# A two-layer streaming encoder step on one core: the row shift of the new values goes through a DRAM scratch instead of an SBUF to SBUF transfer

## The chip, the cores and the metric

One NeuronCore of a Trainium2 chip runs the whole step as one program. The metric is the device time of one execution in microseconds (us), lower is better. It is given as the median of several runs; the profile is one further execution.

## What is computed

Two groups of frames, 2048 prompt frames and 64 sample frames, pass through layer A (attention in a band), then layer B (stick-breaking attention over all earlier keys), each with a gated output projection. Layer B's keys and values come from one projection of the stream between the layers; they are outputs as well:

```
kb, vb = split(rms_norm(x, norm_kv) @ w_kv)              # 2112 x 1024 each
z = q @ k.T * SCALE;  mask = k_pos < q_pos
w = where(mask, exp(log_sigmoid(z) + later), 0)          # later: sum of log_sigmoid(-z) over the keys behind
o = w @ v
y = rms_norm(x + (o * silu(gate)) @ w_out, norm_f)
```

The kernel sums the sticks by parts: it multiplies the running products by the difference of neighbouring value rows, v[t-1] - v[t], and adds the last row at the end. For that it needs each value row beside the row above it. Row t-1 lies in another SBUF partition than row t (a tile holds 128 frames in 128 partitions), so the rows must be moved by one partition; this move is what the change concerns. Row 0 of the prompt has zeros above it, and the first sample frame has the last row of the cache.

## The kernel before

`projections` runs once for each layer, and in each it goes through two halves of the prompt (frames 0 to 1023 with the sample, then 1024 to 2047). Each half has a **value stage** and then a **product stage**.

- The value stage makes V with frames on partitions. A tile is 128 frames (tile 16: the 64 sample frames), and V is made in two halves of 512 columns. `values` does one tile and one half: 24 matmuls into a PSUM bank `ps_v` (16 for the sample tile), one of five banks. The first half of the prompt has 18 such steps, the second 16. Ahead of the product the tile is loaded (`xt`), normed, turned by the TensorE (`ps_tr`) and parted into a high and a low part (`x_own`, in the second half also `big`, `bigl`). In the first pass of the stage, or the second, `mix` forms sums of quarters of x on POOL, DVE and ACT for the product stage.
- The product stage makes K, Q and the gate, transposed, with Strassen-like products (`pair`: seven products of 12 matmuls into `ps_x`, `ps_z`, `ps_y`, which use the same five banks as `ps_v`). `natural` turns finished K chunks back with TensorE (`ps_n`, through `kn`) and writes them to the output `b_k_p`. Staging jobs (cache keys, `stage_diff` for the cache's value differences, the output weights `stage_w_out`) are spread over it.

In layer A `values` splits the PSUM bank straight into `vs` and stores it (`v_a`). In layer B each step does this, on SP unless said otherwise: ACT copies the bank to `vn` (four buffers); `vn` goes to the output `b_v_p` (L413); 127 rows of `vn` go one partition down into `vps` in SBUF (L418); the last row goes to the DRAM scratch `v_raw` (L419), and the row above the tile comes back from it into `vps` row 0 (L425); DVE subtracts `vn` from `vps`; ACT and DVE split the difference into `vs`; `vs` is stored to `v_b` (L396). `vps` has two places, used by turns. The last weight forms of the stage's end (`t4`) take over the place of `vps`.

The order of instructions on each engine is set by the tile framework's scheduler at compile time, unless `order.on` is set, in which case instructions made through the wrapped engines keep the program's order. Waits are put on semaphores, and an engine's queue is strictly in order. SP issues nearly all DMAs of these stages.

Of the kernel before, what the change touches and what calls it, by code (L numbers as in the profile page):

```python
# [16 lines left out]
P = 128  # L17
# [106 lines left out]
def encoder_step(ctx: ExitStack, tc: tile.TileContext, a: dict, o: dict):  # L124
# [143 lines left out]
    def projections(L, x_of, begin, w_v, cv, gv, out_v, jobs, first, prompt, sample, stages):  # L268
        with ExitStack() as own, ExitStack() as beside, ExitStack() as early:
# [98 lines left out]
            marker = {}  # L368

            def values(hf, half, i, t, vws, pool, vps):  # L370
                r0, n = TOK[t]
                xh, xl = xs[hf]
                c = r0 % HALF
                ps = psum.tile([P, CH], F32, name="ps_v", tag="mm", bufs=5)
                out = ps[:n]
                if n == NS:
                    for k in range(NK):
                        mm(ps, x_new[:, k], vws[k][0], start=(k == 0), stop=False)
                        mm(ps, x_new[:, k], vws[k][1], start=False, stop=(k == NK - 1))
                    out = pool.tile([P, CH], F32, name="vn", tag="vn", bufs=VN[L])[:n]  # L380
# [12 lines left out]
                def store(src, to):  # L393
                    vs = pool.tile([P, 8, 2, DH], F32R, name="vs", tag="vs", bufs=2)
                    copied = split(vs[:n, :, 0, :], vs[:n, :, 1, :], src.rearrange("p (h d) -> p h d", d=DH))
                    to(  # L396
                        f32(lay[L]["v"][r0 : r0 + n, heads]),
                        f32(vs[:n]).rearrange("p h s d -> p h (s d)"),
                    )
                    return copied  # L400

                if L == "a":
                    marker[hf, half, i] = store(out, nc.scalar.dma_start)
                dst = out_v(t)
                if dst is None:
                    return
                vn = out
                if n == P:
                    vn = pool.tile([P, CH], F32, name="vn", tag="vn", bufs=VN[L])
                    copied = act.activation(vn, out, AF.Copy)  # L410
                    if L == "b":
                        marker[hf, half, i] = copied
                nc.sync.dma_start(dst[:, cols], vn)  # L413
                if L == "a":
                    return

                prev = vps[i % 2]
                nc.sync.dma_start(prev[1:n], vn[: n - 1])  # L418
                nc.sync.dma_start(vraw[r0 + n : r0 + n + 1, cols], vn[n - 1 : n])  # L419
                if t == 0:  # L420
                    gps.memset(prev[0:1], 0.0)
                elif n == NS:
                    nc.sync.dma_start(prev[0:1], a["cache_b_v"][PAST - 1 : PAST, cols])
                else:
                    nc.sync.dma_start(prev[0:1], vraw[r0 : r0 + 1, cols])  # L425
# [46 lines left out]
            def pair(hf, kind, c0, hp, forms, pool, between):  # L472
# [10 lines left out]
                def plain(ps):  # L483
                    c = pool.tile([P, CH], F32, name="c", tag="c", bufs=CS[L])
                    act.activation(c, ps, AF.Copy)
                    return c

                def leave(b, t0, src):
                    at = slice(r0 + t0 * CH, r0 + t0 * CH + CH)
                    hl = pool.tile([P, 2, CH], F32R, name="hl", tag="hl", bufs=4)  # L490
# [5 lines left out]
                    put(L, kind, hp + b, at, hl)  # L496
                    row = hf * HALF + t0 * CH - first
                    if kind == "k" and row >= 0:
                        natural(pool, src, 0, P, 4, prompt[row : row + CH, (hp + b) * P : (hp + b) * P + P])

                def new_frames():
                    ps = bank("ps_q")[:, : 2 * P]
# [27 lines left out]
                        else:  # L530
                            put(L, kind, hp + b, at, hl[:, b])

                x, y, z = (None,) * 3
# [16 lines left out]
                leave(1, 0, u2)  # L550
                between(3)
                times(x, mixed(hf, 3), t3, False)
                dve.tensor_tensor(c5, x, c5, ALU.add)
# [3 lines left out]
                times(y, quarter(hf, 1, 0), w21, True)  # L557
                dve.tensor_tensor(c1, y, c1, ALU.add)
                leave(0, 0, c1)
                between(5)  # L560
                times(x, quarter(hf, 1, 1), t4, False)
                if kind == "k" and hf * HALF + CH - first >= 0:
                    leave(0, 1, plain(x))
                else:
                    leave(0, 1, x)
                between(6)

            def all_pairs(hf, todo, forms, raws, pool, begun, staging, events):
# [10 lines left out]
                for i, (kind, w, c0, g, hp) in enumerate(todo):  # L579
# [19 lines left out]
                            x()  # L599

                    pair(hf, kind, c0, hp, forms, pool, between)

            def slot(x):
                return x.rearrange("p (i k c) -> p i k c", i=2, k=4)
# [15 lines left out]
            ]  # L620


            seq = [*range(NK), len(TOK) - 1]
            with tc.tile_pool(name=f"v0_{L}", bufs=1) as pool:
                tmp = [x.rearrange("p k (i c) -> p (k i) c", i=2)[:, i] for x in big_parts(F32, (1, 2)) for i in range(4)]
                vps = two_places() if L == "b" else None
# [17 lines left out]
                for i, t in enumerate(seq):  # L644
                    if i + 2 < len(seq):
                        parted(seq[i + 2], turned(seq[i + 2], xts(seq[i + 2])))
                    if i >= 4 and i < 8:
                        mix(0, i - 4, [tmp[0], tmp[4 + i - 4], tmp[1], tmp[2]])
                    values(0, 0, i, t, vws, pool, vps)
                vws = [x for j in range(4) for x in two_blocks(1, j, ring(j), vw(pool))]  # L650
                forms = raws = None
                for i, t in enumerate(seq):
                    values(0, 1, i, t, vws, pool, vps)
                    if 4 <= i < 8:
                        x = tmp[i].rearrange("p (k t) -> p k t", k=4)
                        split(*into(0, 3, i - 4), x)
# [10 lines left out]
                    if i in (5, 6):  # L667
                        steps.pop(0)()
                        steps.pop(0)()
                t4 = opool.tile([P, 2, 4, P], F32R, name="t4", tag="og", bufs=1)  # L670


# [8 lines left out]
            last, seq1, fetched = len(todo[0]) - 1, [*range(NK, 2 * NK)], {}  # L681

            def fetch(part):
                if part == 0:
# [24 lines left out]
            with tc.tile_pool(name=f"v1_{L}", bufs=1) as pool:  # L709
                vps = two_places() if L == "b" else None  # L710
                where = [ahead, ahead, pool]
                for i, t in enumerate(seq1):
                    if i + 2 < NK:
                        home = where[(i + 2) % 3]
                        parted(seq1[i + 2], turned(seq1[i + 2], normed(seq1[i + 2], home, ahead, 1 if home is pool else 2)))
                    values(1, 0, i, t, vws, pool, vps)
                vws = []
                for j in range(4):
                    vws += two_blocks(1, j, "xr", vw(ahead if j < 2 else pool))
# [3 lines left out]
                for i, t in enumerate(seq1):  # L723
                    if i in (0, 2, 4, 6):
                        mix(1, i // 2, tmp)
                    values(1, 1, i, t, vws, pool, vps)
                    if i == 5:
                        raws = [raw_tiles()]
                        b1 = [opool.tile([P, 2, 4, P], F32R, name=f"b1{x}", tag="oh", bufs=2) for x in "hl"]
# [1 line left out]
                        load, scale, _ = weights_of(*todo[1][0], raws[0], [b1, None, None])  # L731
                        load()
                        scale()
                b2 = [opool.tile([P, 2, 4, P], F32R, name=f"b2{x}", tag="ol", bufs=2) for x in "hl"]
            early.close()
            own_forms = beside.enter_context(tc.tile_pool(name=f"st1_{L}", bufs=1))
# [35 lines left out]
        )  # L772


    def stage_diff(t, half, pool):
        cols, heads = slice(half * CH, half * CH + CH), slice(half * 8, half * 8 + 8)
        cur = pool.tile([P, CH], F32, name="vcur", tag="vr", bufs=2)
        prev = pool.tile([P, CH], F32, name="vprev", tag="vp", bufs=2)
        r0 = t * P
        cache = a["cache_b_v"]  # L780
        nc.sync.dma_start(cur, cache[r0 : r0 + P, cols])
        if t:
            nc.sync.dma_start(prev, cache[r0 - 1 : r0 + P - 1, cols])
        else:
            gps.memset(prev, 0.0)
            for x, m in ((0, 112), (112, 15)):
                nc.sync.dma_start(prev[x + 1 : x + 1 + m], cache[x : x + m, cols])

        gps.tensor_tensor(prev, prev, cur, ALU.subtract)
        vs = pool.tile([P, 8, 2, DH], F32R, name="vs", tag="vs", bufs=2)  # L790
        split(vs[:, :, 0, :], vs[:, :, 1, :], prev.rearrange("p (h d) -> p h d", d=DH))
        nc.sync.dma_start(f32(lay["b"]["v"][T + r0 : T + r0 + P, heads]), f32(vs).rearrange("p h s d -> p h (s d)"))


    def stage_w_out(k, half, pool):
# [580 lines left out]
    diffs = [partial(stage_diff, t, i) for t in range(PAST // P) for i in range(2)]  # L1376
    outs_b = [partial(stage_w_out, k, half) for k in range(NK) for half in range(2)]
    staged += keys_b[:8]
    staged_b = [x for i in range(16) for x in (keys_b[8 + i], diffs[16 + i])] + keys_b[24:]
# [18 lines left out]
    with (  # L1398
# [170 lines left out]
        0,  # L1569
        o["b_k_p"],  # L1570
        o["b_k_s"],
        [staged_b, outs_b],
    )

    with (
# [284 lines left out]
```

## Time and profile before

| what | value |
|---|---|
| timed runs | 3604.8 us median (3601.3 to 3606.26, 3 runs) |
| profiled execution, its own time | 3597.26 us |
| its span | 3595.5 us |
| mean granted TensorE clock | 0.947 |
| PE busy / DVE / ACT / POOL | 89% / 63% / 52% / 47% |
| layer B's first value stage, from its first `ps_v` | 1423.0 us |
| layer B's second value stage, from its first `ps_v` | 1992.5 us |

The page's strip of 40 slices shows each engine's busy tenths over time. The windows view gives busy time in chosen stretches, the waits view who waited for whom, the chain of waits the work that ended last, and the timeline every instruction with its start and length. "SPq" is the DMA issue on SP's queue; the length of a "DMA" piece in the chain is from its issue to its landing. Nearly all instructions carry the line of a helper, L113, so groups are told apart by the names of their tiles.

### The profile page before, as it was taken

To read this page: it belongs to the slowest core of one execution; us is meant where nothing else is said; L and a number is where in the kernel's file an instruction comes from. 1 tells how busy PE (TensorE), PEld (TensorE's weight loads), DVE (VectorE), ACT (ScalarE), POOL (GpSimd) and SP (SyncE) were. 2 spreads that over 40 slices of the span, in tenths; PEclk is the share of its full clock that TensorE was granted. 3 is DMA by queue.
4 is the path that set the end of the run, shared out by engine and by line. 5 is a ranking of instruction groups with operands and counts; after the bars stand their busy time and mean duration, and the time that the engine had idled before them with its cause. 6 is when DMAs were issued, how large, how long until landed. Compare 5 with 4: busy or idle time off the path is not lost.

```text
span 3595.5 us, 52143 instructions
## 1 busy us (share of the span) xinstructions
PE 3190.8 (89%) x16760; PEld 2650.4 (74%) x16760; DVE 2247.6 (63%) x3944; ACT 1873.4 (52%) x3743; POOL 1695.6 (47%) x2377
## 2 busy tenths in 40 slices
PE   8999999899989999552999662799999999999999
PEld 6778877688878987441778542578888887888877
DVE  6575466377777743321655322458887788888883
ACT  4445444488877742211544311446666666666662
POOL 4345267256555521311544211424447777777771
PEclk9999999999999999775999876899999999999999
DMA  4776457588999845222988322797683548554423
GB/s 160 249 252 208 149 212 255 170 231 230 258 249 250 225 136 164 82 86 102 344 303 308 137 85 83 270 273 225 187 219 123 146 134 248 148 148 141 123 70 124
DMA packets 470707, 674.72 MB, mean 188 GB/s; under 512 B 60051, under 2 KB 257203, under 8 KB 470434
## 3 DMA queue, kind: packets, MB, share of 16 engines
q1 hardware_dynamic: 425346, 607.95, 55.2%
q10 hardware_dynamic: 45088, 63.45, 5.2%
q8 instruction: 133, 2.18, 0.3%
q14 instruction: 140, 1.15, 0.1%
HBM read 412.51 MB, written 250.18 MB: 184 GB/s over the span
## 4 chain that ended last, share of the span: by engine, by line
PE 31%; DMA 11%; DVE 6%; issue 4%; ACT 2%; POOL 2%; SPq 2%; ACTq 0%; POOLq 0%; DVEq 0%
PE acc L113 6%; PE z L113 6%; PE wt L113 5%; DMA vps<-vn 5%; PE ps_j L113 5%; PE ps_x L113 3%; DMA v_raw<-vn 3%; PE ps_o L113 3%; DVE s L113 2%; DVE pl L113 2%; PE ps_z L113 2%; SPq L419 1%; PE ps_y L113 1%; POOL wraw L113 1%; DMA q<-q_b 1%
## 5 line engine op out<-in xcount | busy, mean ns | idle before, releaser
L113 DVE TENSOR_TENSOR pl<-wt,ph 128x512 fp32r<-128x512 f32 (+1 forms) x864 | 552.0, 655 | 109.4 <-ACT ph L113 105.9
L113 ACT ACTIVATE ph<-wt 128x512 fp32r<-128x512 f32 (+1 forms) x864 | 484.7, 577 | 192.4 <-PE wt L113 178.4
L113 PE MATMUL wt<-ident,s 128*128 128x128 f32 x3472 | 550.1, 274 | 9.4 <-DVE pl L113 7.4
L113 PEld LDWEIGHTS wt<-ident,s 128*128 128x128 f32 x3472 | 417.1, 140 | 84.1 <-DVE pl L113 13.4
L113 ACT ACTIVATE f<-z 128x512 f32<-128x512 f32 (+4 forms) x680 | 355.0, 535 | 191.6 <-PE z L113 129.4
L113 POOL TENSOR_TENSOR s<-f,s 128x256 f32<-128x256 f32 x416 | 360.7, 868 | 101.7 <-DVE s L113 93.6
L113 PE MATMUL z<-kt,q 128*128 128x512 f32 (+3 forms) x1280 | 372.7, 378 | 5.4 <-DMA q<-q_b 2.6
L113 PE MATMUL acc<-ph,vt 128*128 128x512 f32 (+3 forms) x1088 | 374.2, 379 | 3.6 <-ACT ot L113 2.4
L113 PE MATMUL acc<-pl,vt 128*128 128x512 f32 (+3 forms) x1088 | 362.9, 367 | 8.9 <-DVE pl L113 8.5
L113 POOL TENSOR_TENSOR two<-f 128x256 f32<-128x256 f32 x416 | 259.5, 626 | 151.5 <-ACT f L113 136.9
L113 DVE TENSOR_TENSOR_SCAN s<-two,s,own 128x256 f32<-128x256 f32 x408 | 300.3, 739 | 33.5 <-POOL two L113 32.0
L113 POOL TENSOR_SCALAR s<-s,rc 128x640 f32<-128x640 f32 (+5 forms) x264 | 201.2, 767 | 240.8 <-DVE rc L113 140.9
L113 PE MATMUL ps_x<-x_own,t 128*128 128x512 f32 x864 | 221.7, 405 | 68.1 <-DVE t L113 48.5
L113 PEld LDWEIGHTS z<-kt,q 128*128 128x128 f32 x1280 | 220.0, 190 | 36.1 <-ACT f L113 9.8
L113 PEld LDWEIGHTS ps_x<-x_own,t 128*128 128x128 f32 x864 | 163.2, 192 | 110.2 <-ACT c L113 62.8
L113 DVE TENSOR_TENSOR vps<-vps,vn 128x512 f32<-128x512 f32 (+1 forms) x34 | 23.5, 692 | 341.5 <-DMA vps<-vn 291.8
L113 DVE CUSTOM_DVE_ANT_0 s<-z,bias 128x640 f32<-128x640 f32 (+4 forms) x256 | 184.8, 733 | 71.4 <-PE wt L113 54.2
L113 PEld LDWEIGHTS acc<-pl,vt 128*128 128x128 f32 x1088 | 193.7, 190 | 41.6 <-DVE pl L113 25.9
L113 DVE TENSOR_TENSOR_SCAN s<-f,own 128x128 f32<-128x128 f32 (+4 forms) x264 | 202.4, 788 | 29.6 <-ACT f L113 29.2
L113 PEld LDWEIGHTS acc<-ph,vt 128*128 128x128 f32 x1088 | 196.7, 190 | 26.2 <-ACT ph L113 5.4
L113 POOL TENSOR_TENSOR wraw<-wraw 128x512 f32<-128x512 f32 x96 | 146.5, 1539 | 146.9 <-DVE b2l L113 77.8
L113 PE MATMUL ps_o<-big,oh 128*128 128x512 f32 x544 | 213.9, 393 | 0.0
(246 smaller groups left out, 7462.7 us busy)
## 6 DMA issues: line engine op xcount, KB each, us to landing
vt<-v_b SPq DMA_DIRECT2D x80, 512.0 KB
v_b<-vs SPq DMA_DIRECT2D x64, 512.0 KB
q<-q_a SPq DMA_DIRECT2D x128, 256.0 KB
q<-q_b SPq DMA_DIRECT2D x128, 256.0 KB
vt<-v_a SPq DMA_DIRECT2D x48, 512.0 KB
kt<-k_b SPq DMA_DIRECT2D x96, 256.0 KB
keys<-k_a SPq DMA_DIRECT2D x80, 256.0 KB
v_a<-vs ACTq DMA_DIRECT2D x32, 512.0 KB
```

The source lines that it names most:

```text
L113: ins = op(*args, **kwargs)
L419: nc.sync.dma_start(vraw[r0 + n : r0 + n + 1, cols], vn[n - 1 : n])
```

## The change

Three things change; the computation stays the same.

- In layer B `values` writes the whole tile `vn` to `v_raw`, at rows 1 + r0 and on, in place of the last row alone. Nothing is moved between partitions in SBUF. The step leaves two closures, `load` and `less`, in a list; `steps_on`, called after each `values`, calls a tile's `load` (read rows r0 to r0 + 127 of `v_raw` into `vps`) one tile later and its `less` (subtract, split, store) two tiles later, both in program order. What is left is called at the end of the stage.
- For the last two tiles of the second column half in each stage (tiles 7 and 16, then 14 and 15) `values` does no difference at all. `stage_diff` does them as staging jobs in the product stage, reading both `vn` rows and the rows above from `v_raw`; they stand first in the staging lists.
- `natural` is called one product later: `leave` puts it in the list `rows`, and `pair` takes one after its first, fifth, sixth and seventh products (the next pair's too).

```
-                nc.sync.dma_start(prev[1:n], vn[: n - 1])
-                nc.sync.dma_start(vraw[r0 + n : r0 + n + 1, cols], vn[n - 1 : n])
-                if t == 0:
-                    gps.memset(prev[0:1], 0.0)
-                elif n == NS:
-                    nc.sync.dma_start(prev[0:1], a["cache_b_v"][PAST - 1 : PAST, cols])
-                else:
-                    nc.sync.dma_start(prev[0:1], vraw[r0 : r0 + 1, cols])
-                dve.tensor_tensor(prev[:n], prev[:n], vn, ALU.subtract)
-                store(prev[:n], nc.sync.dma_start)
+                nc.sync.dma_start(vraw[1 + r0 : 1 + r0 + n, cols], vn)
+                if half and t in seqs[hf][-2:]:
+                    return
+                def load():
+                    if t == 0:
+                        gps.memset(prev[0:1], 0.0)
+                        for x, m in ((0, 112), (112, 15)):
+                            sp.dma_start(prev[x + 1 : x + 1 + m], vraw[1 + x : 1 + x + m, cols])
+                    elif n == NS:
+                        sp.dma_start(prev[0:1], a["cache_b_v"][PAST - 1 : PAST, cols])
+                        sp.dma_start(prev[1:n], vraw[1 + r0 : r0 + n, cols])
+                    else:
+                        sp.dma_start(prev, vraw[r0 : r0 + P, cols])
+                def less():
+                    dve.tensor_tensor(prev[:n], prev[:n], vn, ALU.subtract)
+                    store(prev[:n], nc.sync.dma_start)
+                waiting.append([1, load, less])
+            def steps_on():
+                was, order.on = order.on, True
+                for x in waiting:
+                    x[0] -= 1
+                    if x[0] < 0:
+                        x.pop(1)()
+                waiting[:] = [x for x in waiting if len(x) > 1]
+                order.on = was
...
-                        natural(pool, src, 0, P, 4, prompt[row : row + CH, (hp + b) * P : (hp + b) * P + P])
+                        rows.append(partial(
+                            natural, pool, src, 0, P, 4, prompt[row : row + CH, (hp + b) * P : (hp + b) * P + P]
+                        ))
...
                 times(x, quarter(hf, 0, 0), w11, True)
+                rows_on()
...
                     values(0, 0, i, t, vws, pool, vps)
+                    steps_on()
...
+                while waiting:
+                    steps_on()
...
-    def stage_diff(t, half, pool):
+    def stage_diff(where, t, half, pool):
...
+            nc.sync.dma_start(cur[:n], vraw[1 + r0 : 1 + r0 + n, cols])
+            if n == P:
+                nc.sync.dma_start(prev, vraw[r0 : r0 + P, cols])
...
+    new_diffs = [partial(stage_diff, "new", t, 1) for t in (7, 16, 14, 15)]
+    staged_b = new_diffs[:2] + [x for i in range(16) for x in (keys_b[8 + i], diffs[16 + i])] + keys_b[24:]
...
-        [staged_b, outs_b],
+        [staged_b, new_diffs[2:] + outs_b],
```

The queue of SP before, in the second column pass of layer B's first value stage. `vn_16285`, `vn_16338` and `vn_16376` are tiles 3, 4 and 5; `vs_16256`, `vs_16292` and `vs_16345` are the split differences of tiles 2, 3 and 4.

```order
L413 DMA out_b_v_p<-vn_16285 128x512
L418 DMA vps_15482<-vn_16285 127x512
L419 DMA v_raw_149<-vn_16285 1x512
L396 DMA v_b_127<-vs_16256 128x1024
L425 DMA vps_15482<-v_raw_149 1x512
L413 DMA out_b_v_p<-vn_16338 128x512
L396 DMA v_b_127<-vs_16292 128x1024
L418 DMA vps_15482<-vn_16338 127x512
L419 DMA v_raw_149<-vn_16338 1x512
L425 DMA vps_15482<-v_raw_149 1x512
```

The same place in the changed kernel. `vn_16319`, `vn_16356` and `vn_16398` are tiles 4, 5 and 6; `vs_16237`, `vs_16272` and `vs_16324` are the differences of tiles 0, 1 and 2. The three reads from `v_raw` are those of tiles 1, 2 and 3.

```order
L414 DMA out_b_v_p<-vn_16319 128x512
L397 DMA v_b_127<-vs_16237 128x1024
L113 DMA vps_15482<-v_raw_149 128x512
L417 DMA v_raw_149<-vn_16319 128x512
L414 DMA out_b_v_p<-vn_16356 128x512
L397 DMA v_b_127<-vs_16272 128x1024
L113 DMA vps_15482<-v_raw_149 128x512
L417 DMA v_raw_149<-vn_16356 128x512
L414 DMA out_b_v_p<-vn_16398 128x512
L397 DMA v_b_127<-vs_16324 128x1024
```

A tile's product was followed by its own shift and, one tile later, its store; now its difference is taken three to four tiles behind its product, and each read from `v_raw` stands right behind the store of the previous tile's difference. There is one DMA fewer for each tile.

DVE before, where the first value stage ends (`vn_16462` is tile 7, `vn_16492` the sample; `t4` and `t3` are weight forms that the first pair needs, `c_16543` is the first pair's own work):

```order
L113 TENSOR_TENSOR vps_15482<-vps_15482,vn_16462 128x512
L113 TENSOR_TENSOR vs_16469<-vps_15482,vs_16469 128x8x64
L113 TENSOR_TENSOR vps_15482<-vps_15482,vn_16492 64x512
L113 TENSOR_TENSOR vs_16500<-vps_15482,vs_16500 64x8x64
L113 TENSOR_TENSOR t4_16504<-wraw_16297,t4_16504 128x512
L113 TENSOR_TENSOR t3_16509<-wraw_16296,t3_16509 128x512
L113 TENSOR_TENSOR c_16543<-ps_y_16708,c_16543 128x512
```

The same place now (`vn_16356` is tile 5, `vn_16398` tile 6):

```order
L113 TENSOR_TENSOR vps_15482<-vps_15482,vn_16356 128x512
L113 TENSOR_TENSOR vs_16445<-vps_15482,vs_16445 128x8x64
L113 TENSOR_TENSOR vps_15482<-vps_15482,vn_16398 128x512
L113 TENSOR_TENSOR vs_16475<-vps_15482,vs_16475 128x8x64
L113 TENSOR_TENSOR t4_16479<-wraw_16278,t4_16479 128x512
L113 TENSOR_TENSOR t3_16484<-wraw_16277,t3_16484 128x512
L113 TENSOR_TENSOR c_16518<-ps_y_16685,c_16518 128x512
```

The weight forms still stand behind the last difference of the stage, which is now that of tile 6 and no longer that of the sample.

More of the change, by code (lines that the diff above doesn't have):

```diff
@@ L366, in vw @@
                 return lambda k: [pool.tile([P, CH], F32R, name=f"vw{x}", tag=f"vw{x}{k}", bufs=1) for x in "hl"]
-            marker = {}
+            marker, waiting, rows = {}, [], []
+            seqs = [[*range(NK), len(TOK) - 1], [*range(NK, 2 * NK)]]
             def values(hf, half, i, t, vws, pool, vps):
@@ L486, in plain, with rows_on @@
                     return c
+                def rows_on():
+                    if rows:
+                        rows.pop(0)()
                 def leave(b, t0, src):
@@ L601, in all_pairs @@
                     pair(hf, kind, c0, hp, forms, pool, between)
+                while rows:
+                    rows.pop(0)()
             def slot(x):
@@ L620, in projections @@
             ]
-            seq = [*range(NK), len(TOK) - 1]
+            seq, seq1 = seqs
             with tc.tile_pool(name=f"v0_{L}", bufs=1) as pool:
@@ L680, in projections @@
             staging = dict(pool=staged.__enter__(), todo=stages[0], until=len(todo[0]) - 2)
-            last, seq1, fetched = len(todo[0]) - 1, [*range(NK, 2 * NK)], {}
+            last, fetched = len(todo[0]) - 1, {}
             def fetch(part):
@@ L733, in projections @@
                         scale()
+                while waiting:
+                    steps_on()
                 b2 = [opool.tile([P, 2, 4, P], F32R, name=f"b2{x}", tag="ol", bufs=2) for x in "hl"]
@@ L1375, in encoder_step @@
     keys_b = [partial(stage_cache, "b", hp, c) for hp in range(HP) for c in range(PAST // CH)]
[L1376 removed]
+    diffs = [partial(stage_diff, "cache", t, i) for t in range(PAST // P) for i in range(2)]
     outs_b = [partial(stage_w_out, k, half) for k in range(NK) for half in range(2)]
     staged += keys_b[:8]
[L1379 removed]
+    new_diffs = [partial(stage_diff, "new", t, 1) for t in (7, 16, 14, 15)]
+    staged_b = new_diffs[:2] + [x for i in range(16) for x in (keys_b[8 + i], diffs[16 + i])] + keys_b[24:]
     jobs_a = [("k", w_a, D, gs["a"]), ("q", w_a, 0, gs["a"]), ("g", w_a, 3 * D, gs["a"])]
```

33 lines of the change are left out of this document (22 added, 11 removed).

## The prediction

> **What bounds the kernel now.** I read the windows view first. Rows one and two are the value stages of layer A, which make the same products without a shift of rows; rows three and four are those of layer B, from the first `ps_v` to the product that the stage's end holds up; the last row is a product stage.
>
> ```profile
> core 0: us, PE busy (x) PEld busy (x) DVE busy (x) ACT busy (x) POOL busy (x), PEclk, DMA share, GB/s
> 10.60:122.00 111.40, 108.51 (x480) 86.23 (x481) 70.86 (x96) 48.94 (x86) 51.23 (x51) 0.98 0.43 155
> 396.40:494.20 97.80, 97.50 (x447) 79.12 (x446) 59.14 (x86) 43.45 (x76) 50.10 (x50) 1.00 0.38 138
> 1423.00:1697.90 274.90, 133.22 (x517) 102.48 (x517) 82.16 (x117) 60.02 (x107) 53.97 (x53) 0.72 0.28 97
> 1992.50:2267.30 274.80, 125.61 (x473) 96.64 (x471) 72.25 (x112) 54.62 (x93) 45.55 (x48) 0.71 0.27 99
> 1700.00:1990.00 290.00, 276.38 (x1346) 224.27 (x1346) 166.16 (x199) 142.18 (x244) 138.95 (x141) 0.98 0.88 310
> ```
>
> Layer A's stages are TensorE's (108.5 of 111.4 us, 97.5 of 97.8). Layer B's take 275 us each; no engine is busy half the time but PE, and PE only because its granted clock is 0.72. DMA is 28% busy. Something is waited for. What PE waits for, in the first stage and then the second (total us, times, longest):
>
> ```profile
> PE ps_x L113 <- ACT c L113: 35.9, 1, 35.9
> PE ps_v L113 <- ACT vwh L113: 26.9, 1, 26.9
> PE ps_y L113 <- ACT vn L113: 23.7, 1, 23.7
> PE ps_tr L113 <- DVE x_own L113: 22.7, 3, 8.4
> PE ps_x L113 <- ACT vn L113: 19.6, 1, 19.6
> ...
> PE ps_x L113 <- DVE t L113: 48.5, 1, 48.5
> PE ps_v L113 <- ACT vwh L113: 26.8, 2, 26.5
> PE ps_y L113 <- ACT vn L113: 17.1, 1, 17.1
> ```
>
> These are ACT and DVE, which are not busy: their queues stand behind something. The chain of waits shows it, here at the first stage's end (start, us, what):
>
> ```profile
> 1641.30 13.09 DMA vps<-vn
> 1654.48 0.70 DVE vps L113
> 1655.80 0.59 ACT vn L113
> 1656.40 0.36 SPq L413
> 1656.82 0.41 SPq L396
> 1657.28 0.63 SPq L418
> 1657.96 17.12 DMA v_raw<-vn
> 1675.10 0.23 SPq L425
> ...
> 1691.33 0.69 DVE vps L113
> 1692.10 0.64 ACT vs L113
> 1692.76 0.69 DVE vs L113
> 1693.47 2.98 DMA v_b<-vs
> ...
> 1697.86 5.49 PE ps_x L113 x12
> ...
> 1708.59 5.59 PE ps_x L113 x24
> ```
>
> One tile is one turn of a ring: shift 254 KB by one partition (13.09 us), subtract, which frees a `vn` buffer, copy the next bank, issue the next shift 16 us after the last (1657.28 against 1641.30). The 2 KB row to `v_raw` takes 17.12 us, since it lies behind the shift, while a 512 KB store to `v_b` lands in 2.98 us. So layer B's value stages are bound by the time of this one transfer, at some 16 us a tile, and PE needs 5.6 us (24 matmuls, the last row above).
>
> **The change part by part.** *The shift and the single row go.* Without them PE's floor would be layer A's windows. First stage: 111.4 us, then what PE does up to the first use of the form t3 (before at 1708.59): three products that stood ahead of 1697.9, 3 x 2.8 = 8.4 us, and 1708.6 - 1697.9 = 10.7 us; the changed order puts two more products ahead of it, 5.6 us. That is 136.1 us against 285.6 + 5.6 us: 155 us to be had. Second stage, to the wait for `t`: 97.8 + 8.4 = 106.2, and about 10 us that stay at its beginning, because a tile of x lands late there:
>
> ```profile
> 2002.11 5.50 DMA xt<-x
> ```
>
> It lands at 2007.6; PE has then been through the two tiles it had (11.2 us from 1992.5, to 2003.7), and norm, turn and split, some 5 us by the turn of the same steps, follow. So 116 us against 274.8: 158 us to be had. Together 313 us: the gain if nothing takes the shift's place.
>
> *A ring of SP's takes its place.* The queue above shows it: a tile's read from `v_raw` stands directly behind the store of the difference of the tile before, and that store waits for DVE, which waits for that tile's read. The read is issued two tiles after its write (a tile is over 5 us, and a store of twice its size lands in 2.98 us), so the write is not waited for. One turn is the read's landing, L, then subtract, split on ACT and on DVE, and the issues of the output, the store and the next read. From the rows above: 1693.47 - 1691.33 = 2.14 us, and 0.36 + 0.41 us of issues, with gaps 3.0 us. Behind SP's wait lie the next tile's output and `v_raw` write; behind DVE's lie the splits of x, and of the next weights.
>
> L isn't in the trace: 256 KB from DRAM in 128 rows, in a stage with 1.25 MB for a tile. The nearest rows: SP issues such a load at 1697.53, behind two others and the `v_b` stores, and POOL, waiting for it and its fellow, starts at 1701.95; on the idle chip 512 KB issued at 0.72 are used at 4.06; in the full product stage (310 GB/s) one takes 6.77 us.
>
> ```profile
> 1697.53 0.44 SPq L783 DMA_DIRECT2D vprev<-in_cache_b_v  x1
> ...
> 1701.95 1.27 POOL L113 TENSOR_TENSOR vprev<-vprev,vcur 128x512 f32<-128x512 f32 x1 [1.72 <-DMA vcur<-in_cache_b_v]
> ```
>
> ```profile
> 0.72 0.39 SPq L321 DMA_DIRECT2D xt<-in_x_prompt  x1
> ...
> 4.06 1.06 ACT L113 ACTIVATE junk<-xt 128x1024 bf16<-128x1024 f32 x1 [2.06 <-DMA xt<-in_x_prompt]
> ```
>
> ```profile
> 1723.19 6.77 DMA vprev<-in_cache_b_v
> ```
>
> So L is 3.3 to 6.8 us; I take 4.4, the row with a store ahead of the load, as here. A turn is 7.4 us (6.3 to 9.8): longer than PE's 5.6, half of today's 16.
>
> The ring starts when the second tile is out, about 1.5 us after these issues:
>
> ```profile
> 1446.47 0.45 SPq L413 DMA_DIRECT2D out_b_v_p<-vn  x1
> ...
> 2008.39 0.40 SPq L413 DMA_DIRECT2D out_b_v_p<-vn  x1
> ```
>
> First stage: 16 reads (18 steps less the two that are put off), 1448 + 16 x 7.4 = 1566, and 4 us for the forms t4 and t3 behind it (now the `v_b` issue at 1693.47 to 1697.86 is 4.4): 1570, against 1708.6 + 5.6 = 1714.2. Saved 144 us; PE alone would be ready at 1559. The `vn` and PSUM buffers, four and five, let PE run this far ahead. Second stage: 14 reads, 2010 + 14 x 7.4 = 2113.6, and 5.3 us from the last store's issue to the product that waits for `t`, as now:
>
> ```profile
> 2262.02 2.96 DMA v_b<-vs
> ...
> 2267.34 4.35 PE L113 MATMUL ps_x<-x_own,t 128*128 128x512 f32 x12 [48.55 <-DVE t L113]
> ```
>
> So 2119 against 2267.3: 148 us. Other DVE work (mixing) stands between subtract and split in about a third of the tiles: 10 x 0.69 = 7 us back. The ring saves 144 + 148 - 7 = 285 us.
>
> *Four differences move into the product stages.* Each loads 512 KB and stores 512 KB: 1 MB at the 310 GB/s of the windows row, 3.3 us of DMA, there 88% busy, and about 1.3 us each on POOL, ACT and DVE. PE, at 276 of 290 us, hides most: I take 1.5 us each, 6 in all (0 to 13).
>
> *`natural` a product later.* What it can win is what PE waits for around it in the product stage:
>
> ```profile
> PE ps_n L113 <- ACT kn L113: 4.7, 2, 3.0
> PE ps_q L113 <- ACT kn L113: 3.1, 2, 2.4
> ```
>
> At most 8 us, at worst nothing lost but a `c` buffer held for one more product (2.8 us); I take 1 us.
>
> Sum: 285 - 6 + 1 = 280 us. The profiled execution's own 3597.3 becomes 3317. The median of the timed runs is 7.5 us above it, so 3604.8 - 280 = 3325 us.
>
> **The rivals.** *Nothing takes its place.* If a read lands in 2.6 us or less, the turn is PE's 5.6, and the stages come near layer A's: 313 - 5 = 308 us, 3297. For it: DMA was only 28% busy. Against: no load in the trace is that short. The Trainium skill, DMA: Bandwidth & Descriptors, section Anatomy of one DMA, fits 2.0 us plus bytes over 436 GB/s (measured on the software path), 2.6 us for this read, by estimate; the trace's 3.3 us for 512 KB on an idle chip is just that rule, but here a store lies ahead.
>
> *Slow reads.* With the 1.25 MB of each tile in the rings, L is that of the full product stage, 6.8 us: 30 reads x 2.4 = 72 us less, 208 saved, 3397. For it: each read follows a 512 KB store at once. Against: 1.25 MB in 7.4 us is 170 GB/s, little over half of the 310 at which 6.8 was measured.
>
> *The write is waited for.* If scratch writes land late, a read waits for its own: some 3 us more in each turn (the 2.98 us row), 30 x 3 = 90 us less, 190 saved, 3415. The order speaks against it: two tiles lie between. The same section of that page says that the completion of a write to HBM can take surprisingly long, which speaks against a way through scratch; the 2.98 us row doesn't show it.
>
> *Slower than before.* If the read were as slow as the shift, because its rows too go through one DMA engine, a turn would be 14 + 3 = 17 us, where today's is 16: 30 us lost, 3635. It decides from L of 13 us on, where a turn is today's. For it: what makes the shift slow is not in its size (254 KB in 13.09 us against 512 KB in 2.98). Against: loads of the same shape, 128 rows of 2 KB, take 4.4 to 6.8 us. The Trainium skill has a rule for it (same page, section Why a DMA increments its semaphore by 16 and not by 1): a transfer runs on the largest number of engines up to 16 that divides its rows, 127 rows on one and 128 on sixteen. By that rule the rival falls; the trace agrees with it for 127 rows.
>
> **How the numbers follow.** The ring on SP with 250 to 300 us saved: 0.62. Nothing takes its place (over 300): 0.14. Slow reads (210 to 250): 0.15. The write waited for, or another wait that keeps most of the gain away: 0.06. Slower: 0.02. No change that can be told: 0.01. About 0.2%, 7 us, is what a measurement of this kernel can tell. So faster 0.97. The range: 3290 is 315 saved, the whole floor with 2 us of `natural`; 3390 is 215, slow reads in nearly all turns; what lies outside is the last three cases and the edges of the others, some 0.15.
>
> **What would show it.** Right: no `vps<-vn`; the first stage about 145 us from `ps_v` to t3, the second about 127; reads 7 to 8 us apart on SP, each right behind a `v_b` store; landing 4 to 5 us; PE's clock near 1 in these stages. Wrong: reads under 6 us apart and PE without waits (the ring isn't there); SP waiting for `v_raw` writes; waits for `vprev` or `kn` in the product stages that eat more than 10 us; or stages longer than 170 us.

## The result, and the profile after

| | before | after |
|---|---|---|
| timed runs, median | 3603.05 us (3600.33 to 3606.26) | 3357.15 us (3350.82 to 3360.76) |
| ratio | 1 | 0.9315, 95% interval 0.9297 to 0.9333 |
| profiled execution, own time / span | 3597.26 / 3595.5 us | 3359.73 / 3357.9 us |
| mean granted TensorE clock | 0.947 | 0.979 |

The change saves 246 us; 280 were forecast. The direction, the place and the mechanism came out as argued; the ring on SP (a tile's read, its difference, the store of that, and only then the next read) is longer than it was taken to be.

Where the time went is told by the windows view, here for layer B's value stages: from the first `ps_v` to the first product with the form t3 in the first stage, and from the first `ps_v` to the first product of `big` with `t` in the second. Before:

```profile
core 0: us, PE busy (x) PEld busy (x) DVE busy (x) ACT busy (x) POOL busy (x), PEclk, DMA share, GB/s
1423.00:1708.40 285.40, 143.72 (x560) 111.22 (x561) 85.23 (x121) 63.18 (x112) 59.98 (x63) 0.72 0.29 101
1992.50:2284.30 291.80, 141.91 (x543) 109.61 (x542) 80.68 (x123) 61.99 (x105) 56.34 (x62) 0.73 0.31 111
```

After, the same two stages, and then the first stage's stretch in which DVE also mixes sums of quarters of x:

```profile
1429.50:1596.30 166.80, 135.93 (x587) 105.83 (x587) 90.09 (x119) 62.20 (x111) 63.13 (x62) 0.93 0.59 190
1884.40:2049.20 164.80, 123.95 (x541) 99.42 (x540) 85.03 (x120) 61.38 (x102) 67.02 (x68) 0.89 0.65 223
...
1456.00:1495.00 39.00, 34.68 (x149) 27.48 (x148) 37.91 (x45) 18.09 (x36) 25.00 (x17) 0.91 0.40 136
```

The stages are 118.6 and 127.0 us shorter, 245.6 together. The engines do much the same work (PE even has two more products ahead of the first stage's mark); what went is waiting, and with it the low granted clock (0.72 to 0.93 and 0.89). In the last row DVE is busy 37.9 of 39 us.

The reads of the changed kernel, by the group of the tile `vps`, and SP's queue in the second column pass of the first stage (start, length of the issue, line, what):

```profile
L113 SPq DMA_DIRECT2D vps<-v_raw x32: 319/425/702, 1453.1 to 2017.8; - x32
...
DMA to landing us min/median/max: 2.4/4.1/6.2
```

```profile
1508.29 0.33 SPq L397 DMA_DIRECT2D v_b<-vs  x1
1508.66 0.42 SPq L113 DMA_DIRECT2D vps<-v_raw  x1
1509.18 0.74 SPq L414 DMA_DIRECT2D out_b_v_p<-vn  x1
1509.97 0.50 SPq L417 DMA_DIRECT2D v_raw<-vn  x1
1514.65 0.32 SPq L397 DMA_DIRECT2D v_b<-vs  x1
1515.02 0.42 SPq L113 DMA_DIRECT2D vps<-v_raw  x1
```

Each read stands right behind the store of the tile before, as forecast; these two are 6.4 us apart, and a read lands in 4.1 us where 4.4 were taken. DVE at the same place, and then where it mixes (the bracket is its idle time before, and who ended it):

```profile
1506.12 0.69 DVE L113 TENSOR_TENSOR vps<-vps,vn 128x512 f32<-128x512 f32 x1 [0.78 <-DMA vps<-v_raw]
1507.57 0.69 DVE L113 TENSOR_TENSOR vs<-vps,vs 128x512 fp32r<-128x512 f32 x1 [0.75 <-ACT vs L113]
1512.49 0.69 DVE L113 TENSOR_TENSOR vps<-vps,vn 128x512 f32<-128x512 f32 x1 [4.23 <-DMA vps<-v_raw]
```

```profile
1456.69 0.68 DVE L113 TENSOR_TENSOR vps<-vps,vn 128x512 f32<-128x512 f32 x1
...
1460.35 0.93 DVE L113 TENSOR_TENSOR vs<-vps,vs 128x512 fp32r<-128x512 f32 x1
1461.21 1.77 DVE L113 TENSOR_TENSOR big<-bigl,big 128x512 fp32r<-128x512 f32 x1
1462.90 1.77 DVE L113 TENSOR_TENSOR bigl<-bigl,bigl 128x512 fp32r<-128x512 f32 x1
...
1468.10 2.29 DVE L113 TENSOR_TENSOR big<-bigl,big 128x512 fp32r<-128x512 f32 x1
1470.31 0.68 DVE L113 TENSOR_TENSOR vps<-vps,vn 128x512 f32<-128x512 f32 x1
1470.91 2.32 DVE L113 TENSOR_TENSOR bigl<-bigl 128x512 f32<-128x512 f32 x2
```

In the first place DVE waits for the read, and the subtractions are 6.4 us apart. In the second it never idles: the split into `vs` comes 3.7 us behind its subtraction, not 1.5, and the next subtraction 13.6 us behind this one. Over the whole stages the subtractions lie 8.31 us apart (16 of them, 1456.69 to 1581.40) and 8.32 us (14, 1914.33 to 2022.51).

What PE waited for longest in the first stage, and then in the second (total us, times, longest):

```profile
PE ps_x L113 <- ACT c L113: 15.4, 1, 15.4
PE ps_x L113 <- ACT b1h L113: 4.9, 1, 4.9
```

```profile
PE ps_x L113 <- DMA vcur<-in_w_out_b: 31.6, 1, 31.6
PE ps_tr L113 <- POOL xt L113: 6.1, 1, 6.1
```

PE was through with the tiles long before the ring was, and stood 15.4 and 31.6 us at the stages' ends. The releaser named in the second is only the last to arrive by the profile's count; the chain that ends at PE there runs through the ring's last turn, its store's landing and ACT's copy into `t` behind it:

```profile
2023.25 0.62 ACT vs L113
...
2023.90 0.70 DVE vs L113
...
2024.62 3.58 DMA v_b<-vs
...
2028.27 0.42 ACT t L113
```

### The profile page after: what moved, and what is told of

The parts are those of the page before. It is cut to its first block, busy times and chain, and to the rows that moved or that the text cites. A ratio compares the mean times of both kernels' runs of the same rounds, so it can differ in the third digit from the quotient of the medians.

```text
span 3357.9 us, 52063 instructions
## 1 busy us (share of the span) xinstructions
PE 3167.8 (94%) x16760; PEld 2636.3 (79%) x16760; DVE 2252.1 (67%) x3940; ACT 1873.6 (56%) x3743; POOL 1705.9 (51%) x2381
## 5 line engine op out<-in xcount | busy, mean ns | idle before, releaser
L113 POOL TENSOR_SCALAR s<-s,rc 128x640 f32<-128x640 f32 (+5 forms) x264 | 201.1, 767 | 245.6 <-DVE rc L113 145.5
L113 PE MATMUL ps_x<-x_own,t 128*128 128x512 f32 x864 | 222.4, 406 | 51.7 <-DMA vcur<-in_w_out_b 31.6
L113 ACT ACTIVATE s<-s,mn 128x640 f32<-128x640 f32 (+5 forms) x264 | 200.2, 760 | 28.0 <-DVE mn L113 24.7
```

The source lines that it names most:

```text
L113: ins = op(*args, **kwargs)
```

## The experiments

All are timed against the kernel before on the same chip (medians of 3599.3 to 3600.4 us there; the table's first two rows are the pair above, and each ratio is to its own chip's runs). The stages are measured between the marks above, in us, from the profiles: V1 and V2 are the value stages, P1 the product stage between them, rest what follows.

| kernel | V1 | P1 | V2 | rest | median us | ratio, 95% interval |
|---|---|---|---|---|---|---|
| before | 285.4 | 284.1 | 291.8 | 1311.2 | 3603.05 | 1 |
| after | 166.8 | 288.1 | 164.8 | 1308.7 | 3357.15 | 0.9315 (0.9297 to 0.9333) |
| after again (e11) | 168.4 | 286.8 | 166.4 | 1308.7 | 3354.16 | 0.9311 (0.9298 to 0.9324) |
| read ahead of the store (e1) | 143.7 | 288.9 | 135.7 | 1312.9 | 3310.75 | 0.9191 (0.9174 to 0.9208) |
| the same, places by turns (e5) | 140.9 | 286.2 | 137.8 | 1313.5 | 3304.01 | 0.9179 (0.9164 to 0.9195) |
| reads on ACT (e2) | 143.1 | 288.2 | 138.7 | 1310.4 | 3311.18 | 0.9194 (0.918 to 0.9207) |
| before, shift in two (e3) | 144.3 | 285.6 | 151.5 | 1306.1 | 3320.54 | 0.922 (0.9206 to 0.9233) |
| after, reads of 127 rows (e4) | 296.4 | 284.8 | 298.2 | 1307.4 | 3614.07 | 1.0038 (1.0026 to 1.005) |
| `natural` in place (e6) | 164.8 | 288.0 | 164.4 | 1304.7 | 3348.01 | 0.9301 (0.9286 to 0.9317) |
| all differences in the stage (e7) | 179.3 | 284.5 | 183.9 | 1301.9 | 3376.6 | 0.9378 (0.9364 to 0.9392) |
| after, shift in two in SBUF (e8) | 138.4 | 282.5 | 146.7 | 1311.5 | 3308.22 | 0.9194 (0.9177 to 0.921) |
| after, `mix` without adds (e9) | 157.2 | 282.4 | 156.4 | 1307.9 | 3330.68 | 0.9249 (0.9236 to 0.9262) |
| e5, `natural` in place (e10) | 141.1 | 280.6 | 137.9 | 1314.7 | 3300.07 | 0.9161 (0.9149 to 0.9174) |
| e8, `natural` in place (e12) | 140.0 | 289.1 | 145.7 | 1312.7 | 3313.0 | 0.9204 (0.9191 to 0.9216) |

### Is it the ring? Reads taken out of it, and the ring made shorter

e1: the list of waiting closures is gone through from the newest, so that SP has a tile's read ahead of the store of the tile before. Where the second column pass begins, two differences in a row then use the same place of `vps`, and one sample tile's difference is lost.

```
-                for x in waiting:
+                for x in reversed(waiting):
                     x[0] -= 1
```

> The changed kernel, but on SP each read from v_raw now stands ahead of the v_b store of the tile before instead of right behind it (the closures in the list are taken from the newest to the oldest). A read then waits only for the difference two tiles back, so two reads are in flight. Theory (the ring of one read, subtract, split, store, next read sets the pace, at 8.3 and 9.0 us a tile): reads come about 6 us apart in the undisturbed places, TensorE's 5.6 us is the bound, and the time falls by 30 to 55 us, to 3302 to 3327. Rival A (DVE's other work and the late loads of x set the pace, not the order on SP): 3350 to 3365, no change. Rival B (a read one place closer to its own write must wait for it): a read's landing grows by 2 us or more and the time rises above 3365.

3310.75 us. The first stage gets 23 us shorter and the second 29. (The changed kernel's turns are 8.31 and 8.32 us on the mean, not 8.3 and 9.0 as the text above has it.) The edit was then made again with the two places of `vps` taken strictly by turns:

```
-                prev = vps[i % 2]
+                place = marker['vps'] = marker.get('vps', -1) + 1
+                prev = vps[place % 2]
```

> As the kernel with the read ahead of the store of the tile before; there, where the first column pass ends and the second begins, two differences in a row used the same place of vps (nine steps in the pass), so one sample tile's difference was overwritten. Here the places are taken strictly by turns. Theory (two reads in flight take the ring away, and that fault was no part of the gain): 3303 to 3318. Rival (a part of the gain came from the step that did not wait at the border): 3325 to 3345.

3304.01 us, so the fault was no part of the gain. The windows of its two stages, between the same marks:

```profile
1426.20:1567.10 140.90, 129.61 (x580) 102.03 (x581) 89.95 (x118) 62.60 (x111) 65.30 (x65) 0.99 0.68 229
1853.30:1991.10 137.80, 120.31 (x529) 96.88 (x529) 81.73 (x114) 57.18 (x96) 63.54 (x63) 0.93 0.68 237
```

The ring was the bound: with two reads in flight the subtractions lie 6.48 and 6.26 us apart on the mean, near the 5.6 us that PE needs, though DVE and ACT are busy for as long as in the changed kernel, within 5 us. The first stage, 140.9 us, comes within 5 us of the floor that the prediction had worked out for a kernel without any ring (136.1). PE's wait of 15.4 us at the first stage's end is gone, and the 31.6 us at the second's have become 9.4 (e5, its longest waits in the first stage and then in the second):

```profile
PE ps_v L113 <- ACT vwh L113: 5.1, 1, 5.1
PE ps_x L113 <- ACT c L113: 9.4, 1, 9.4
```

e2 leaves one read at a time, but issues it from ACT:

```
-                        sp.dma_start(prev, vraw[r0 : r0 + P, cols])
+                        act.dma_start(prev, vraw[r0 : r0 + P, cols])
```

> The changed kernel with its reads from v_raw issued by ACT, right behind ACT's split of the tile before, in place of SP, right behind the v_b store. The ring stays (one read at a time) but loses the DVE split (0.7 us) and two issues on SP (0.8 us). Theory (the length of that ring is the pace): 28 turns that are 1.0 to 1.5 us shorter, 28 to 42 us, so 3315 to 3330; less than the kernel in which two reads are in flight, or as much if TensorE then bounds both. Rival (the pace is set by DVE's other work or by loads of x): 3350 to 3365.

3311.18 us, a little more gain than the theory gave. Besides the DVE split and the two issues, the turn has lost a part of the landing: the read no longer stands right behind a 512 KB store on SP's queue, and its median landing is 3.0 us in place of 4.1.

```profile
DMA to landing us min/median/max: 2.5/3.0/7.1
```

The subtractions lie 6.65 and 6.39 us apart. The Trainium skill, DMA: Bandwidth & Descriptors, section Anatomy of one DMA, gives this read an estimate of 2.6 us by its fit, which was measured on the software path. The shortest here took 2.5 us, the median behind a store 4.1.

### Was it the way through scratch, or the number of rows?

e3 is the kernel before, with one edit:

```
-                nc.sync.dma_start(prev[1:n], vn[: n - 1])
+                for x, m in ((0, 112), (112, 15)) if n == P else ((0, n - 1),):
+                    nc.sync.dma_start(prev[x + 1 : x + 1 + m], vn[x : x + m])
```

> The kernel before, still moving rows from SBUF to SBUF by one partition, but each shift of 127 rows is made as two transfers, of 112 rows and of 15. Theory (the shift was slow because of its 127 rows, which one DMA engine carries, not because it stays in SBUF or crosses partitions): the shift lands in 4 to 6 us in place of 13.1, and a turn of before's ring, 16 us, becomes about 8; the time falls to between 3340 and 3400. Rival (moving rows between partitions inside SBUF is slow in itself, and the way through scratch is what helps): 3560 to 3605.

3320.54 us, below the whole range that was expected: this one edit to the kernel before gives more than the change does. The chain of waits shows why. The shift of 254 KB that took 13.09 us now goes in two parts that land like other transfers:

```profile
1494.36 3.53 DMA vps<-vn
1513.80 2.53 DMA vps<-vn
1522.78 4.16 DMA vps<-vn
...
1977.26 3.50 DMA vps<-vn
```

e4 asks the reverse of the changed kernel:

```
-                        sp.dma_start(prev, vraw[r0 : r0 + P, cols])
+                        sp.dma_start(prev[0:1], vraw[r0 : r0 + 1, cols])
+                        sp.dma_start(prev[1:P], vraw[1 + r0 : r0 + P, cols])
```

> The changed kernel, with each read of 128 rows from v_raw made as one of 1 row and one of 127. Theory (127 rows go through one DMA engine): the read of 127 rows lands in 13 to 17 us, as the shift did, a turn is 17 to 20 us, and nearly all of the gain is lost or more: 3590 to 3680. Rival (the shift's slowness was not in the number of rows; what makes the changed kernel fast is that rows come from DRAM): 3350 to 3375.

3614.07 us: the whole gain is lost, and 0.4% more. The chain now goes from read to read, 18 to 19 us a turn here, though no row moves inside SBUF:

```profile
1601.07 14.70 DMA vps<-v_raw
1618.95 16.18 DMA vps<-v_raw
1638.38 14.75 DMA vps<-v_raw
1656.83 14.65 DMA vps<-v_raw
```

The two runs settle it: 127 rows are slow from SBUF (13.1 us) and from DRAM (14.2 to 16.6 us in the chain of e4); 128 rows from DRAM (4.1 us) and 112 and 15 rows within SBUF (1.7 to 4.2 us) are quick. The way through scratch is not what helps.

The traces also show why. These rows of the windows view are the shift of 127 rows before, the read of 127 rows in e4, each while hardly anything else is on its way, and the changed kernel with a read of 128 rows and the store ahead of it:

```profile
1650.20:1654.00 3.80, 0.00 (x0) 0.00 (x0) 0.00 (x0) 0.00 (x0) 0.00 (x0) 0.50 0.07 26
1680.00:1688.50 8.50, 0.00 (x0) 0.00 (x0) 0.00 (x0) 0.00 (x0) 0.00 (x0) 0.50 0.07 26
1509.40:1512.40 3.00, 3.00 (x15) 2.41 (x14) 0.00 (x0) 0.00 (x0) 0.00 (x0) 1.00 0.97 320
```

A DMA share of 0.07 is the time of one of the core's 16 DMA engines; at 26 GB/s, 254 KB take 10.0 us, most of the 13.1. In the last row all 16 are busy nearly all the time. The rule that the prediction named (the Trainium skill, DMA: Bandwidth & Descriptors, section Why a DMA increments its semaphore by 16 and not by 1) is that a transfer takes the largest number of engines up to 16 that divides its rows: 16 for 112, 15 for 15, one for 127. The share agrees with it for 127 rows, the landings for the others.

e8 puts the split shift into the changed kernel, with its four moved differences and the later `natural`; `load` and `less` go.

```
-                waiting.append([1, load, less])
+                for x, m in ((0, 112), (112, 15)) if n == P else ((0, n - 1),):
+                    nc.sync.dma_start(prev[x + 1 : x + 1 + m], vn[x : x + m])
...
+                dve.tensor_tensor(prev[:n], prev[:n], vn, ALU.subtract)
+                store(prev[:n], nc.sync.dma_start)
```

> The changed kernel, but the rows are moved inside SBUF at once, as before, by two transfers of 112 and 15 rows; the four moved differences and the later `natural` stay. Beside the kernel before with only the split shift (3320.5) it tells what those two parts are worth once the ring is short. Theory: TensorE waited 7.9 and 21.1 us at the ends of the stages there; without the last two turns these go, and the four staging jobs cost about 10 us: 3298 to 3315. Rival (the jobs and the later `natural` cost what the ends give): 3316 to 3330. Against the changed kernel (3357) it also tells whether the way through scratch is worth anything: if it is, this kernel is slower than 3357.

3308.22 us: 46 to 49 us quicker, by the medians, than the way through scratch as the change has it (e11 and the pair above), and 12 us quicker than e3 (the intervals of the two ratios just overlap).

### The two smaller parts

e7 takes the moved differences back into the stage.

```
-                if half and t in seqs[hf][-2:]:
-                    return
...
-    staged_b = new_diffs[:2] + [x for i in range(16) for x in (keys_b[8 + i], diffs[16 + i])] + keys_b[24:]
+    staged_b = [x for i in range(16) for x in (keys_b[8 + i], diffs[16 + i])] + keys_b[24:]
...
-        [staged_b, new_diffs[2:] + outs_b],
+        [staged_b, outs_b],
```

> The changed kernel with the last two differences of each stage done in the stage again, none as a staging job. Theory (the ring on SP sets the stage's end): two more turns for the first stage (one of them the sample's, half as long) and two for the second, 8 us each, about 28 us, less 6 to 11 us that the product stages no longer do: 3370 to 3385. Rival (what is moved costs as much where it goes): 3350 to 3362.

3376.6 us. The two stages grow by 12.5 and 19.1 us, and 3.6 and 6.8 us come back in what follows them. Moving the differences is worth some 20 us with this ring; the jobs cost about 10 of the 32 that the ring gets shorter.

e6, e10 and e12 call `natural` at once, in the changed kernel, in e5 and in e8:

```
-                        rows.append(partial(
-                            natural, pool, src, 0, P, 4, prompt[row : row + CH, (hp + b) * P : (hp + b) * P + P]
-                        ))
+                        natural(pool, src, 0, P, 4, prompt[row : row + CH, (hp + b) * P : (hp + b) * P + P])
```

> The changed kernel with `natural` called at once again, not a product later. Theory (it is nearly nothing, as predicted: 1 us, at most 8): 3349 to 3365. Rival A (turning keys at once makes TensorE wait for the copy kn, in each of the products that leave a chunk): 3365 to 3390, so the deferral was part of the gain. Rival B (the deferral holds back the next buffer c): 3335 to 3349.

> The kernel with two reads in flight and places taken by turns (3304), and `natural` called at once. Theory (the later `natural` costs a few us wherever it is, as the 9 us between 3357 and 3348 hint): 3294 to 3301. Rival (it is worth nothing that can be told): 3301 to 3310.

> The kernel that moves rows inside SBUF by two transfers, with the four moved differences (3308), and `natural` called at once: what is left of the change is the moved differences. Theory: as with two reads in flight, a few us less, 3298 to 3306. Rival (no difference): 3306 to 3314.

3348.01, 3300.07 and 3313.0 us: 6 to 9 us less than the changed kernel, 4 less than e5, 5 more than e8. The intervals of the ratio overlap in each pair, and the signs differ. The later `natural` is worth less than 10 us either way; which way stays open. e10 has the lowest median of the study, 0.9161 of before.

### What makes the turns longer than 7.4 us

e9 leaves DVE's four adds out of each `mix` in layer B (the first of the four is shown):

```
-                dve.tensor_tensor(a22, a21, a22, ALU.add)
+                if L == "a":
+                    dve.tensor_tensor(a22, a21, a22, ALU.add)
```

> The changed kernel with the four adds on DVE left out of each `mix` of layer B (32 adds; the sums of quarters are then not formed, so layer B's K, Q and gate are made from wrong numbers; all other work stays). The subtractions of neighbouring tiles lie 8.3 us apart on the mean in the changed kernel, 6.2 to 8 where nothing disturbs, 9 to 13.6 where DVE also mixes. Theory (DVE's other work stands in the ring's turns, and that is the term of the sum that was too small): the turns in the stretches with mixing get 1 to 2 us shorter, the stages together 8 to 20 us, 3337 to 3349. Rival (the long turns are those in which a tile of x, ACT or POOL is late): 3350 to 3362.

> The changed kernel itself on the same chip as these, to compare with directly: 3350 to 3361.

The changed kernel again gave 3354.16 us, e9 3330.68: 23.5 us less, more than expected. The first turn of the stage with mixing falls from 13.2 us (in e11) to 8.5, all turns on the mean from 8.40 and 8.51 to 7.60 and 7.72, and the same 39 us in which DVE was busy 37.9 now show half of it:

```profile
1456.00:1495.00 39.00, 37.27 (x173) 29.64 (x172) 19.05 (x30) 17.96 (x34) 13.98 (x11) 1.00 0.53 176
```

So DVE's other work stood in the ring's turns. With these 32 adds away, the turns come within 0.2 and 0.3 us of the 7.4 that the prediction had for a ring of the transfer and its own steps alone.

## Why the prediction was right, and where its sum was off

- **The bound.** That layer B's value stages hang on one transfer was right, and e3 shows it in the barest form: only that transfer is changed, and 279 us go. The prediction gave the reason for its slowness, one DMA engine for 127 rows, only inside a rival. It is what e3, e4 and the share of 0.07 show, and the way through scratch is not needed for the gain.
- **The ring on SP.** Right: e2 and e5 shorten or open it and gain 43 to 50 us against e11. The landing was right (4.1 us for 4.4), and so was the turn where nothing disturbs it (mostly 6.2 to 8.2 us for 7.4). The other signs came out short of the forecast: the stages are 166.8 us to t3 and 145.7 to `t`, where about 145 and 127 were given, and the granted clock is 0.93 and 0.89, not near 1.
- **The term that was mis-sized** is "7 us for other DVE work standing in the turns". The turns measured 8.31 and 8.32 us; over 7.4 that is 13.7 us in the first stage's 15 turns and 12.0 in the second's 13, 25.7 together. The prediction allowed one operation of 0.69 us in a third of the tiles. Where `mix` runs, DVE has no idle time and each operation of the ring stands behind several others, some of which take two to three times 0.69 us (see the last section); e9 shows that this work is what lengthens the turns. A ring that is longer than PE's 5.6 us can't make up for a late turn; in e5 the same mixing goes on and turns of 8 to 13 us come too, but later turns of 3.2 to 5.2 us make up for them.
- **Two ends, 8 us each.** In the second stage the first subtraction came 29.9 us behind the first `ps_v` (1884.4 to 1914.33), where 17.5 + 4.4 = 21.9 were taken. The read was issued in time, at 1900.28; DVE's queue had the splits of the next tiles of x (`bigl`) ahead of the subtraction:

```profile
1911.73 0.15 DVE L113 TENSOR_SCALAR ms<-ss 128x1 f32<-128x1 f32 x1 [2.36 <-ACT junk L113]
1912.14 0.69 DVE L113 TENSOR_TENSOR bigl<-ps_tr,big 128x512 fp32r<-128x512 f32 x1 [0.26 <-ACT big L113]
1913.65 0.75 DVE L113 TENSOR_TENSOR bigl<-ps_tr,big 128x256 fp32r<-128x256 f32 x2 [0.82 <-ACT big L113]
1914.33 1.21 DVE L113 TENSOR_TENSOR vps<-vps,vn 128x512 f32<-128x512 f32 x1
```

  In the first stage 14.9 us lie between the last subtraction (1581.40) and t3 (1596.26), where 7.0 were taken; ACT's second copy into `t` waits for the last `v_b` store to land, ACT frees a bank for PE only behind it, and PE, which goes on at 1587.61, still has three products ahead of t3:

```profile
1581.40 0.69 DVE L113 TENSOR_TENSOR vps<-vps,vn 128x512 f32<-128x512 f32 x1 [4.15 <-DMA vps<-v_raw]
...
1586.97 0.69 DVE L113 TENSOR_TENSOR t<-wraw,t 128x512 fp32r<-128x512 f32 x1 [2.06 <-ACT t L113]
```

```profile
1586.31 0.63 ACT L113 ACTIVATE t<-wraw 128x512 fp32r<-128x512 f32 x1 [2.12 <-DMA v_b<-vs]
1586.96 0.60 ACT L113 ACTIVATE c<-ps_x 128x512 f32<-128x512 f32 x1
```

- **The balance between the two profiles.** 25.7 + 8.0 + 7.9 us, less 2.9 at the other two ends, is 38.7 where 7 stood: 31.7 less saved. The product stage behind the first value stage, with the 5.6 us that moved ahead of its mark, takes 9.6 us more than before where 5 were taken (6 for the jobs less 1 for `natural`): 4.6. Behind t in the second stage 2.1 us are lost and later 2.5 won. The first `ps_v` comes 6.5 us later than before, in a part of the program that the change doesn't touch; in the other runs it lies anywhere from 1421.2 to 1431.5. 280 - 31.7 - 4.6 - 2.1 + 2.5 - 6.5 = 237.6, the difference of the two spans.
- **The moved differences.** Costed at 6 us, bounds 0 to 13: e7 shows 10 back in the product stages.
- **The rivals.** "Nothing takes its place", 3297, is what the change becomes with two reads in flight (3304.01). "Slower", 3635 by a turn of 17 us, is e4: turns of 16.9 and 18.2 us on the mean, 3614.07. "Slow reads" fell: 190 and 223 GB/s in the stages left the landing at 4.1 us. The saving of 246 us lies in the band of 210 to 250 that was meant for this rival, but for another reason, the longer turns. "The write is waited for" fell too; SP's waits have one such in the first stage (below) and one of 2.1 us in the second, and with a read one place nearer to its write (e5) the time fell:

```profile
SPq L113 <- DMA v_raw<-vn: 2.9, 1, 2.9
```

## What to carry to other kernels

When a transfer of ordinary size is many times slower than its neighbours, look at the DMA share while it runs alone; if it is that of one engine, split the transfer into counts of rows that many engines can share before rerouting it; one edit to the kernel before gave more than the whole rebuilt path. When a read stands behind a store on a queue in strict order, follow the store back to what it waits for: where that is the last read's own consumer, put the read ahead of the store and give it a second buffer. Price such a ring with all that the shared engine does in those microseconds, since a ring longer than the bound's pace keeps every delay.

## What the runs showed of the hardware

- An elementwise DVE operation on 128x512 that reads SBUF alone can take two to three times as long while POOL works. In the two stages of the changed kernel, 172 such two-input operations were counted. All 31 that took over 0.9 us (up to 2.29) overlap a POOL operation and read no PSUM bank; the 81 that read SBUF alone and overlap none took at most 0.70 us, the 28 that read a PSUM bank at most 0.69, though 21 of these overlap one. (The other 32 overlap one too and took no longer than 0.9 us.) The 31 took 25.5 us more than at 0.69 us each. In the stretch with mixing above, the two operations of 1.77 us run under this one:

```profile
1460.71 6.82 POOL L113 TENSOR_TENSOR bigl<-x_own,x_own 128x512 f32<-128x512 f32 x4
```

  No run here takes POOL's work away, so the link is by overlap alone, and how much of the 25.5 us is in the ring's turns is not shown.
- A shift by one partition inside SBUF, in two transfers, lands in 1.7 to 4.2 us (12 pieces of the chain in e3, one of the two transfers each): moving rows between partitions costs no more than reading them back from DRAM (2.4 to 6.2 us).
- The granted clock followed the waiting and not the work: 0.72 where PE waited for half of a stage, 0.99 in e5's first stage with the same products.
